# Folded statistics, transposed row spreads and split float32r sums with borrowed buffers, in a two-block kernel on one core

## The chip, the cores and the metric

One core of a Trainium2 chip runs the kernel. The metric is device time in microseconds (us). The core has a matrix engine (TensorE, PE in the profile, with its weight loads shown apart as PEld), a vector engine (VectorE, DVE), an activation engine (ScalarE, ACT), a general engine (GpSimd, POOL) and an engine that issues transfers (SyncE, SP). TensorE reads SBUF and writes PSUM.

## The reference, cut to what matters

The input is 256 tokens of 1024 features. The first block has three branches that read the same normalised input: a recurrence (RWKV), a stick-breaking attention and an attention over a memory. Their outputs are gated, projected, summed, and followed by a convolutional feed-forward part. The second block is an mLSTM layer, a feed-forward part, an attention layer and another feed-forward part. Every layer begins with an RMS norm. The lines that the change touches compute this:

```
def rms_norm(x, g, eps=NORM_EPS):
    y = x * lax.rsqrt(jnp.mean(x * x, axis=-1, keepdims=True) + eps)
    return y * g

# stick-breaking attention, per head
log_1mb = jnp.where(mask, jax.nn.log_sigmoid(-z), 0.0)
log_between = lax.cumsum(log_1mb, axis=3, reverse=True) - log_1mb
attn = jnp.where(mask, jnp.exp(jax.nn.log_sigmoid(z) + log_between), 0.0)

# merging the branches
gates = jax.nn.sigmoid(gate_logits.reshape(b, t, N_BRANCH, D_MODEL))
merged = jnp.sum(gates * jnp.einsum('btnc,ncd->btnd', ys, w_branch), axis=2)

# mLSTM: the decay matrix of a chunk is built from running sums bcum of log forget gates
dmat = jnp.where(tri, bcum[..., :, None] - bcum[..., None, :] + ib[..., None, :], -jnp.inf)
```

## The kernel before

**Layout.** Features lie on partitions, tokens on the free axis. Each weight matrix is streamed from HBM in pieces of 128 x 1024 in one fixed order. ScalarE rounds a piece to a high half in float32r (L237) and VectorE subtracts to get the low half (L238). A product of weights and activations is three float32r products, high by high, high by low and low by high (L340 to L342, or L363 to L365 where tokens lie on partitions). There are three buffers for the high and three for the low halves of pieces, so TensorE can't run further ahead in the stream than three pieces of eight 128 x 128 weight tiles. Small products that need full precision are plain float32.

**Order.** Each engine runs its own list in order. The lists are not in the order of the program text: a scheduler places the instructions by its own estimates of when operands and buffers are ready, and text that comes later fills waits of text that comes earlier. Tiles are taken from pools. A pool hands out one buffer for each tag, tiles that name the same tag share it in turn, and a tile without a tag uses its own name as the tag. A later tile's first write then waits for the last reader of the earlier tile.

**RWKV** (`run_rwkv`) keeps the operands of its chunks in the tiles `rw_sc` (SC), `rw_rb` (RB) and `rw_z` (Z). After an inversion of triangular blocks (L722, six groups) comes a loop over four chunks, each dependent on the last: products `rw_pp` with SC (L745), copies to SBUF (L748, L749), `rw_puu` with Z (L755), copies (L756, L757), the state product `rw_pS` (L764) and its scaling (L769, or L772 and L775), and products with RB into the same bank (L786). In the last chunk SC, Z and RB are read for the last time.

**Stick-breaking** runs four rounds, p = 0 to 3, each for two heads. A round computes scores `sb_z` (L896), masks them (L899), takes the softplus in `e` by three activations (L900 to L902) and a vector operation (L903), forms running sums over key positions as float32 products of `e` with a triangular constant, `sb_c` (L907 to L909), adds them to z (L910), takes the exponential (L911), multiplies by the values, `sb_o` (L916, L918), and splits the result into `yB` (L311, L312). Its working tile `sb_ze` has one buffer, so a round begins when the one before has ended.

**Gates and branches** (L927 to L940) run over n = memory, stick-breaking, RWKV, and in each over eight tiles m. One m takes a gate product of eight k (24 matmuls on `x1`) and a branch product of four k (12 matmuls on `yM`, `yB` or `yA`); k = p of `yB` comes out of round p. The weight stream has this very order, gate m, branch m, gate m + 1, and so on; the output projection and all later layers follow it.

**Statistics.** `Stats` collects squares of the stream in two 128 x 256 halves. `_rows` sums them over partitions by products with a column of ones (L429), and `_spread` brings the 1/rms of 128 tokens, a column, to a row on all partitions by a product with the identity (L440). In the mLSTM part (L1062 to L1091) `ml_pc` holds two sets of small transposes that make columns, and `ml_pm` spreads one row per head over 128 partitions by a product with four-row operands (L1086).

Of the kernel before, what the change touches and what calls it, by code (L numbers as in the profile page):

```python
# [24 lines left out]
FINE = 16  # the first pieces of weights are split by quarters: short chains share the vector engine  # L25

STARTS = (82, 148, 181, 247, 279)  # likewise the pieces where a layer starts
HEAD = 4  # tiles of an up projection that leave the last two steps of k for later


# ---------------------------------------------------------------- host layout
# [153 lines left out]
# ---------------------------------------------------------------- device side  # L185
# [5 lines left out]
def body(tc, a, out, voff, coff, tap=None, upto=99):  # L191
# [26 lines left out]
    # ---- the weight stream: [128, 1024] pieces, each split into two float32r halves  # L218
# [41 lines left out]
    # ---- inputs that stay  # L260
# [40 lines left out]
    # the tensor engine's clock comes up while the first operands arrive  # L301
# [25 lines left out]
    class Half:  # L327
        """hi and lo of 512 features in one piece"""
# [27 lines left out]
    def tp_group(X):  # L356
        """512 columns with tokens on partitions: two banks"""
        po = [ps_acc(), ps_acc()]
        for k in range(KD):
            hi, lo = W.take(4)  # L360
            for tt in range(2):
                s = slice(tt * 128, (tt + 1) * 128)
                PE.matmul(po[tt], X.H[:, k, s], hi, start=(k == 0), stop=False)  # L363
                PE.matmul(po[tt], X.L[:, k, s], hi, start=False, stop=False)  # L364
                PE.matmul(po[tt], X.H[:, k, s], lo, start=False, stop=(k == KD - 1))  # L365
        return po

    def rsqrt(v, n, name, E=V, out=None):
        """1/sqrt(v) of a small [128, n] tile, v > 0: a first guess from the exponent, a step with fitted
        constants that leaves 7e-4, then one of third order"""  # L370
        c = "r" if name[:2] == "rw" else "x"
        w = spool.tile([128, 4 * n], F32, name=name + "w", tag=f"nw{n}{c}")
        y, t, z, p = [w[:, i * n:(i + 1) * n] for i in range(4)]
        c1 = 0.703952253 * 0.375
        E.tensor_scalar(y.bitcast(I32), v.bitcast(I32), -0.5, float(0x5F1FFFF9), op0=OP.mult, op1=OP.add)
        E.tensor_tensor(t, y, y, op=OP.mult)
        E.tensor_tensor(t, t, v, op=OP.mult)
        E.tensor_scalar(t, t, -c1, c1 * 2.38924456, op0=OP.mult, op1=OP.add)
        E.tensor_tensor(z, t, y, op=OP.mult)
        E.tensor_tensor(t, z, z, op=OP.mult)  # L380
        y = out if out is not None else y
        if E is G:
            E.tensor_tensor(t, t, v, op=OP.mult)
            E.tensor_scalar(t, t, 64.0 / 9, -5.0 / 3, op0=OP.mult, op1=OP.add)
            E.tensor_tensor(p, t, t, op=OP.mult)
            E.tensor_scalar(p, p, 20.0 / 9, None, op0=OP.add)
            E.tensor_tensor(y, p, z, op=OP.mult)
        else:
            E.scalar_tensor_tensor(t, t, 64.0 / 9, v, op0=OP.mult, op1=OP.mult)
            E.scalar_tensor_tensor(p, t, -10.0 / 3, t, op0=OP.add, op1=OP.mult)  # L390
            E.scalar_tensor_tensor(y, p, 5.0, z, op0=OP.add, op1=OP.mult)
        return y

    class Stats:
        """mean of squares of a feature-major [128, 8, 256] stream, tile by tile"""
# [5 lines left out]
        def add(self, x2):  # L401
            """two tiles"""
            sq = spool.tile([128, 2, T], F32, name="st_sq", tag="st_sq", bufs=2)
            A.activation(sq, x2, AF.Square)
            if self.acc is None:
                self.acc = sq
            elif self.n == 1:
                n = spool.tile([128, 2, T], F32, name="st_acc", tag="st_acc", bufs=1)
                self.E.tensor_tensor(n, self.acc, sq, op=OP.add)
                self.acc = n  # L410
            else:
                (self.E if self.n < 3 else V).tensor_tensor(self.acc, self.acc, sq, op=OP.add)
            self.n += 1
# [10 lines left out]
        def _rows(self):  # L424
            nm = self.name
            p = ps_m("st_ps")
            for tt in range(2):
                for j in range(2):
                    PE.matmul(p[:, tt:tt + 1], self.acc[:, j, tt * 128:(tt + 1) * 128], ones[:, 0:1], start=(j == 0),  # L429
                              stop=(j == 1))  # L430
            self.v = spool.tile([128, 2], F32, name=nm + "_v", tag="st_v", bufs=4)
            V.tensor_scalar(self.v, p[:, 0:2], 1.0 / D, EPS, op0=OP.mult, op1=OP.add)
            self.rs = rsqrt(self.v, 2, nm, G, spool.tile([128, 2], F32, name=nm + "_rs", tag="st_rs", bufs=4))
            self.ev = spool.tile([128, 2], F32, name=nm + "_ev", tag="st_ev", bufs=4)
            V.tensor_scalar(self.ev, self.v, EPS, None, op0=OP.mult)

        def _spread(self):
            pb = ps_m("st_pb")
            for tt in range(2):
                PE.matmul(pb[:, tt * 128:(tt + 1) * 128], self.rs[:, tt:tt + 1].to_broadcast([128, 128]), ident,  # L440
                          start=True, stop=True)
            self.bc = spool.tile([128, T], F32, name=self.name + "_bc", tag="st_bc", bufs=2)
            A.activation(self.bc, pb[:, :T], AF.Copy)
            self.bc2 = self.bc[:, None, :].to_broadcast([128, 2, T])

    def head_rs(po, nh, ev, name):
        """rows [tok, nh heads] of two banks -> their 1/sqrt(mean + eps * v)"""
# [21 lines left out]
    def tok_to_feat(qn, dst, tt, gain):  # L469
        """[128 tok, 512] -> dst [128 feat, 4, 256] with a gain per feature"""  # L470
# [6 lines left out]
    # =============================================================== block 1  # L477
# [30 lines left out]
    # normalised already: its rows go to many places  # L508
# [10 lines left out]
    # ---- RWKV  # L519
    half_w0 = cpool.tile([128, 8], F32, name="half_w0")  # L520
    V.tensor_scalar(half_w0, vecs[:, voff["w0"][0]:voff["w0"][0] + 8], 0.5, None, op0=OP.mult)
    # -k_k, k_a / 2, 1 - k_a / 2, 1 - mu; columns of 0.5 and of the decay's factor
# [48 lines left out]
    def rw_norms():  # L571
        """1/|k| of every row and head"""
# [11 lines left out]
    def rw_prep(p, rs, SC, BK, UV, wc):  # L584
        """one pair of heads: decays, keys and values into the operands of the chunks"""
# [51 lines left out]
    def rw_scores(p, SC, BK, BA, RB, BKT, Lb):  # L637
        """scores of a pair of heads; transposes of its B, K and of its strictly lower part"""
# [23 lines left out]
    def run_rwkv():  # L662
# [17 lines left out]
        # (I - L)^-1 of all chunks and heads, both orientations  # L680
# [5 lines left out]
        # diagonal blocks of 16: one block per partition, inverted row by row  # L686
# [50 lines left out]
        # chunks  # L737
# [52 lines left out]
        # group norm  # L790
# [39 lines left out]
    # emission: first projections, half 0 as soon as its six tiles are there  # L830
# [14 lines left out]
    # ---- memory branch: attention  # L845
# [39 lines left out]
    # ---- stick-breaking branch  # L885
    skT = qk_feat(X1, None, 8, vec("sb_k"), "skT")
    sv = v_tok(X1, None, "sv")
    YB = Half("yB", "e")
    for p in range(4):
        ze = mp.tile([128, 4, 384], F32, name="sb_ze", tag="sbt")  # L890
        z, e = ze[:, 0:2], ze[:, 2:4]
        pz = [ps_m("sb_z") for _ in range(2)]
# [10 lines left out]
        V.scalar_tensor_tensor(e, z, 0.0, e, op0=OP.max, op1=OP.add)  # L903
        for par in range(2):
            ep = e[:, par]
            pc = ps_m("sb_c")
            PE.matmul(pc[:, 0:256], con("negtri"), ep[:, 0:256], start=True, stop=False, skip_group_check=True)  # L907
            PE.matmul(pc[:, 128:256], con("negtri")[:, 0:1].to_broadcast([128, 128]), ep[:, 256:384], start=False, stop=True, skip_group_check=True)
            PE.matmul(pc[:, 256:384], con("negtri"), ep[:, 256:384], start=False, stop=True, skip_group_check=True)  # L909
            V.tensor_tensor(z[:, par], z[:, par], pc[:, :384], op=OP.add)  # L910
# [12 lines left out]
    # ---- gates and branches  # L923
# [18 lines left out]
    def residual(X, gains_next, snext, Xn, kn=KD, two=False):  # L942
        """x += W X; the next layer's split input and statistics along the way"""
# [89 lines left out]
    # =============================================================== block 2: mLSTM  # L1033
# [12 lines left out]
    # log_sigmoid(f) = min(f, 0) - ln(1 + exp(-|f|))  # L1046
# [15 lines left out]
    # columns: g (by key position) and the floor of the denominator (by query position)  # L1062
    gcol = mp.tile([128, 2, 2, 4], F32, name="ml_gcol")
    pc = ps_m("ml_pc")
    pcv = pc[:, 0:16].rearrange("p (r a h) -> p r a h", r=2, h=4)
    for r in range(2):
        for tt in range(2):
            PE.transpose(pcv[:, r, tt], rows[:, r, tt * 128:(tt + 1) * 128], ident[0:4, 0:4])
# [15 lines left out]
    for h in range(4):  # L1084
        pm = ps_m("ml_pm")
        PE.matmul(pm[:, :T], ident[0:4, h:h + 1].to_broadcast([4, 128]), rows[:, 2], start=True, stop=True)  # L1086
# [79 lines left out]
    # =============================================================== block 2: attention  # L1166
# [33 lines left out]
    def mb_scores(g):  # L1200
        qT, kT = qk_[g]
        for h in range(4):
# [17 lines left out]
            # [s0,t0] [s0,t1] [s1,t1]  # L1220
# [60 lines left out]
```

## Time and profile before

| What | Value |
|---|---|
| Median of 3 runs | 1159.06 us (1157.35 to 1160.1) |
| Profiled execution, first to last instruction | 1156.9 us |
| Median of the runs less this span | 2.16 us |
| TensorE busy | 1143.2 us, 99% of the span |
| VectorE busy | 864.9 us, 75% |
| ScalarE busy | 663.7 us, 57% |
| Mean granted TensorE clock | 0.998 of full |

The profile comes from one execution; its own whole time is not listed apart from its span, so a sum made against the span is carried to the runs by the 2.16 us that lie around it. An engine's busy time is the union of its instructions' times. Matmuls overlap in the records, so the price of one is read from the distance between starts, not from its length.

### The profile page before, as it was taken

The numbers are of one execution on the slowest core, as the hardware profiler recorded it, in microseconds if no ns is written. First come the engines' busy times: TensorE is split into PE (matmuls) and PEld (weight loads), VectorE is DVE, ScalarE is ACT, GpSimd is POOL, SyncE is SP. The second block draws the span as 40 slices with busy tenths as digits, with TensorE's granted clock in tenths as the row PEclk, the third lists the DMA queues.
The fourth block names the chain that finished last, engine by engine and source line by source line (L and its number), as shares of the span: only waits on it lengthen the run. The fifth ranks groups of instructions, "written<-read, shape, count | busy, mean of one in ns | idle before, by whom it ended". The sixth has DMA issues, their size and how long they took to land.

```text
span 1156.9 us, 22629 instructions
## 1 busy us (share of the span) xinstructions
PE 1143.2 (99%) x8970; PEld 1079.9 (93%) x8970; DVE 864.9 (75%) x1636; ACT 663.7 (57%) x1132; POOL 51.7 (4%) x131
## 2 busy tenths in 40 slices
PE   8999999999999999999999999999999999999998
PEld 6897769999999999999979999999998899999998
DVE  7767877456767999866656779998669858999943
ACT  6745455364545766644546666665455656766632
POOL 2000000010001000000100010000010002000000
PEclk9999999999999999999999999999999999999999
DMA  7544333223466565666554656555655435555563
GB/s 283 183 143 130 93 101 73 93 87 114 130 222 201 169 186 183 186 176 193 165 173 132 182 166 197 185 181 174 192 190 182 152 122 168 183 182 183 182 202 109
DMA packets 60794, 189.37 MB, mean 164 GB/s; under 512 B 12688, under 2 KB 14992, under 8 KB 60688
## 3 DMA queue, kind: packets, MB, share of 16 engines
q1 hardware_dynamic: 59792, 186.51, 51.9%
q8 instruction: 70, 1.15, 0.4%
q0 software_dynamic: 320, 1.05, 0.3%
q10 hardware_dynamic: 576, 0.37, 0.1%
q14 instruction: 36, 0.29, 0.1%
HBM read 186.46 MB, written 1.44 MB: 162 GB/s over the span
## 4 chain that ended last, share of the span: by engine, by line
PE 96%; ACT 2%; DVE 1%; DMA 0%; issue 0%; SPq 0%; ACTq 0%
PE acc L340 24%; PE acc L341 24%; PE acc L342 24%; PE acc L363 4%; PE acc L364 4%; PE acc L365 4%; ACT whi L237 1%; PE tr L473 1%; PE rw_pp L745 1%; PE rw_ps L646 1%; PE rw_lt L722 1%; PE rw_lz L722 1%; PE sb_z L896 1%; PE rw_pvt L630 1%; DMA mst<-in_memT_dram 0%; PE st_ps L429 0%
## 5 line engine op out<-in xcount | busy, mean ns | idle before, releaser
L237 ACT ACTIVATE whi<-wstg 128x1024 fp32r<-128x1024 f32 (+1 forms) x453 | 374.4, 851 | 345.6 <-PE acc L341 189.3
L238 DVE TENSOR_TENSOR wlo<-wstg,whi 128x1024 fp32r<-128x1024 f32 (+1 forms) x453 | 429.6, 967 | 174.6 <-ACT whi L237 172.1
L340 PE MATMUL acc<-ffh,whi 128*128 128x256 f32 x528 | 148.5, 283 | 0.0
L341 PE MATMUL acc<-ffl,whi 128*128 128x256 f32 x528 | 148.1, 283 | 0.0
L342 PE MATMUL acc<-ffh,wlo 128*128 128x256 f32 x528 | 147.7, 283 | 0.0
L340 PEld LDWEIGHTS acc<-ffh,whi 128*128 128x128 f32 x528 | 101.2, 192 | 0.0
L341 PEld LDWEIGHTS acc<-ffl,whi 128*128 128x128 f32 x528 | 100.9, 192 | 0.0
L342 PEld LDWEIGHTS acc<-ffh,wlo 128*128 128x128 f32 x528 | 100.7, 192 | 0.0
L341 PE MATMUL acc<-x6l,whi 128*128 128x256 f32 x352 | 99.3, 284 | 0.8 <-DVE x6l L315 0.8
L340 PE MATMUL acc<-x2h,whi 128*128 128x256 f32 x352 | 99.4, 283 | 0.0
L340 PE MATMUL acc<-x6h,whi 128*128 128x256 f32 x352 | 99.3, 283 | 0.0
L340 PE MATMUL acc<-x4h,whi 128*128 128x256 f32 x352 | 99.2, 283 | 0.0
L341 PE MATMUL acc<-x2l,whi 128*128 128x256 f32 x352 | 99.2, 283 | 0.0
L341 PE MATMUL acc<-x4l,whi 128*128 128x256 f32 x352 | 99.2, 283 | 0.0
L342 PE MATMUL acc<-x2h,wlo 128*128 128x256 f32 x352 | 98.1, 283 | 0.0
L342 PE MATMUL acc<-x4h,wlo 128*128 128x256 f32 x352 | 98.1, 283 | 0.0
L342 PE MATMUL acc<-x6h,wlo 128*128 128x256 f32 x352 | 98.0, 283 | 0.0
L340 PE MATMUL acc<-x1h,whi 128*128 128x256 f32 x304 | 88.0, 291 | 2.8 <-ACT mv L496 1.9
L342 PE MATMUL acc<-x1h,wlo 128*128 128x256 f32 x304 | 87.4, 289 | 0.6 <-DVE wlo L238 0.6
L341 PE MATMUL acc<-x1l,whi 128*128 128x256 f32 x304 | 87.1, 288 | 0.0
L1007 ACT ACTIVATE ffa<-ffu,ffcv 128x256 f32<-128x256 f32 x132 | 70.8, 588 | 0.0
L341 PEld LDWEIGHTS acc<-x6l,whi 128*128 128x128 f32 x352 | 67.5, 192 | 1.2 <-DVE x6l L315 1.2
(587 smaller groups left out, 2825.1 us busy)
## 6 DMA issues: line engine op xcount, KB each, us to landing
wstg<-in_wst_dram SPq DMA_DIRECT2D x343, 512.0 KB, 3.7
wstg<-in_wst_dram SPq DMA_DIRECT2D x4, 256.0 KB, 5.2
mst<-in_memT_dram SPq DMA_DIRECT2D x4, 256.0 KB, 5.7
x<-in_xT_dram SPq DMA_DIRECT2D x2, 512.0 KB, 7.7
xt<-in_xT_dram POOLq DMA_DIRECT2D x4, 256.0 KB, 5.5
out_dram<-xt SPq DMA_DIRECT2D x8, 128.0 KB, 3.7
cst<-in_cst_dram SPq DMA_DIRECT2D x1, 673.0 KB, 8.3
small<-in_small_dram SPq DMA_DIRECT2D x1, 512.0 KB, 8.9
```

Source lines behind the costliest of these rows:

```text
L237: A.activation(hi[:, p], src[:, p], AF.Copy)
L238: V.tensor_tensor(lo[:, p], src[:, p], hi[:, p].bitcast(F32), op=OP.subtract)
L340: PE.matmul(o, hi, xh, start=start, stop=False, **kw)
L341: PE.matmul(o, hi, xl, start=False, stop=False, **kw)
L342: PE.matmul(o, lo, xh, start=False, stop=stop, **kw)
L363: PE.matmul(po[tt], X.H[:, k, s], hi, start=(k == 0), stop=False)
L364: PE.matmul(po[tt], X.L[:, k, s], hi, start=False, stop=False)
L365: PE.matmul(po[tt], X.H[:, k, s], lo, start=False, stop=(k == KD - 1))
L473: PE.transpose(p[:, j * 128:(j + 1) * 128], qn[:, j * 128:(j + 1) * 128], ident)
L630: PE.matmul(pv4[64:128, c], pv[:, c * 64:(c + 1) * 64], ident, start=True, stop=True)
L722: PE.matmul(ps[s, u], l[s, u], r[s, u], start=True, stop=True)
L1007: A.activation(ac[:, g], u[:, g, 2:], AF.Identity, scale=cv[:, c + 2:c + 3], bias=cv[:, c + 3:c + 4])
```

## The change

The sums over partitions in `_rows` are made of one half: VectorE first adds the second half of the squares to the first, and then one product per 128 tokens stands where two stood. `_spread` and the mLSTM's `ml_pm` use a TensorE transpose of a column repeated 128 times in place of a float32 product with the identity; for `ml_pm` the column of the third row set is taken from `ml_pc`, which gets two more small transposes, and a larger copy `ml_gcol`. In the stick-breaking part `e` is split into two float32r halves `eh` and `el`, the triangular constant and its first column, repeated, are copied to float32r (`ntri`, `none`), and the running sums are four float32r products: two of 384 columns and two of 128. The new tiles name tags of RWKV tiles: `sb_nr` has `rw_z`, `sb_el` has `rw_sc`, `sb_eh` has `rw_rb`. Comments and a few documentation strings go too.

```diff
         def _rows(self):
             nm = self.name
             p = ps_m("st_ps")
+            V.tensor_tensor(self.acc[:, 0], self.acc[:, 0], self.acc[:, 1], op=OP.add)
             for tt in range(2):
-                for j in range(2):
-                    PE.matmul(p[:, tt:tt + 1], self.acc[:, j, tt * 128:(tt + 1) * 128], ones[:, 0:1], start=(j == 0),
-                              stop=(j == 1))
+                PE.matmul(p[:, tt:tt + 1], self.acc[:, 0, tt * 128:(tt + 1) * 128], ones[:, 0:1], start=True, stop=True)
...
         def _spread(self):
             pb = ps_m("st_pb")
             for tt in range(2):
-                PE.matmul(pb[:, tt * 128:(tt + 1) * 128], self.rs[:, tt:tt + 1].to_broadcast([128, 128]), ident,
-                          start=True, stop=True)
+                PE.transpose(pb[:, tt * 128:(tt + 1) * 128], self.rs[:, tt:tt + 1].to_broadcast([128, 128]), ident)
...
     YB = Half("yB", "e")
+    nr = mp.tile([128, 2, 128], F32R, name="sb_nr", tag="rw_z")
+    ntri, none = nr[:, 0], nr[:, 1]
+    A.activation(ntri, con("negtri"), AF.Copy)
+    A.activation(none, con("negtri")[:, 0:1].to_broadcast([128, 128]), AF.Copy)
     for p in range(4):
         ze = mp.tile([128, 4, 384], F32, name="sb_ze", tag="sbt")
         z, e = ze[:, 0:2], ze[:, 2:4]
+        el = mp.tile([128, 2, 384], F32R, name="sb_el", tag="rw_sc")
+        eh = mp.tile([128, 2, 384], F32R, name="sb_eh", tag="rw_rb")
...
         V.scalar_tensor_tensor(e, z, 0.0, e, op0=OP.max, op1=OP.add)
+        split(eh, el, e)
         for par in range(2):
-            ep = e[:, par]
             pc = ps_m("sb_c")
-            PE.matmul(pc[:, 0:256], con("negtri"), ep[:, 0:256], start=True, stop=False, skip_group_check=True)
-            PE.matmul(pc[:, 128:256], con("negtri")[:, 0:1].to_broadcast([128, 128]), ep[:, 256:384], start=False, stop=True, skip_group_check=True)
-            PE.matmul(pc[:, 256:384], con("negtri"), ep[:, 256:384], start=False, stop=True, skip_group_check=True)
+            PE.matmul(pc[:, 0:384], ntri, eh[:, par], start=True, stop=False, skip_group_check=True)
+            PE.matmul(pc[:, 0:384], ntri, el[:, par], start=False, stop=False, skip_group_check=True)
+            PE.matmul(pc[:, 128:256], none, eh[:, par, 256:384], start=False, stop=False, skip_group_check=True)
+            PE.matmul(pc[:, 128:256], none, el[:, par, 256:384], start=False, stop=True, skip_group_check=True)
             V.tensor_tensor(z[:, par], z[:, par], pc[:, :384], op=OP.add)
...
-    gcol = mp.tile([128, 2, 2, 4], F32, name="ml_gcol")
+    gcol = mp.tile([128, 3, 2, 4], F32, name="ml_gcol")
     pc = ps_m("ml_pc")
-    pcv = pc[:, 0:16].rearrange("p (r a h) -> p r a h", r=2, h=4)
-    for r in range(2):
+    pcv = pc[:, 0:24].rearrange("p (r a h) -> p r a h", r=3, h=4)
+    for r in range(3):
...
         pm = ps_m("ml_pm")
-        PE.matmul(pm[:, :T], ident[0:4, h:h + 1].to_broadcast([4, 128]), rows[:, 2], start=True, stop=True)
+        for tt in range(2):
+            PE.transpose(pm[:, tt * 128:(tt + 1) * 128], gcol[:, 2, tt, h:h + 1].to_broadcast([128, 128]), ident)
```

## Rows read from the trace of the kernel before

**Rows 1.** The page, busy time, share of span and instructions of an engine.

```profile
PE 1143.2 (99%) x8970; PEld 1079.9 (93%) x8970; DVE 864.9 (75%) x1636; ACT 663.7 (57%) x1132; POOL 51.7 (4%) x131
```

**Rows 2.** Busy time of the engines in stretches: length, then PE, PEld, DVE, ACT, POOL (records), clock, DMA.

```profile
30.00:36.00 6.00, 4.13 (x20) 3.16 (x19) 6.00 (x21) 6.00 (x19) 0.26 (x1) 1.00 0.58 160
36.00:39.40 3.40, 3.40 (x18) 3.40 (x18) 2.51 (x10) 1.35 (x5) 1.62 (x3) 0.50 0.58 199
...
251.00:285.00 34.00, 34.00 (x335) 31.32 (x334) 19.85 (x33) 18.14 (x27) 1.84 (x2) 1.00 0.29 95
```

**Rows 3.** Tile views of `yB`, `yA`: count, shortest, median, longest (ns), first and last start.

```profile
L340 PE MATMUL acc<-yB,whi x32: 283/283/388, 260.9 to 301.1; 128*128 128x256 f32 x32
L312 DVE TENSOR_TENSOR yB<-sb_o,yB x4: 423/424/426, 202.4 to 266.8; 128x256 fp32r<-128x256 f32 x4
L342 PE MATMUL acc<-yA,wlo x32: 282/283/283, 310.9 to 339.5; 128*128 128x256 f32 x32
```

**Rows 4.** Tile views of `rw_z`, `rw_sc`, `rw_rb`: their readers in the chunk loop.

```profile
L755 PE MATMUL rw_puu<-rw_pc,rw_z x64: 218/218/267, 232.1 to 279.1; 64*64 64x64 f32 x64
L745 PE MATMUL rw_pp<-rw_uv,rw_sc x64: 218/275/323, 226.7 to 272.7; 128*128 128x64 f32 x64
L786 PE MATMUL rw_pp<-rw_uv,rw_rb x64: 218/218/267, 235.8 to 283.6; 64*64 64x64 f32 x64
```

**Rows 5.** Timeline of TensorE, running sums and the last chunk: start, length (us).

```profile
190.55 0.59 PE L907 MATMUL sb_c<-sb_ze,cst 128*128 128x256 f32 x2
191.42 0.60 PE L907 MATMUL sb_c<-sb_ze,cst 128*128 128x256 f32 x2
...
238.17 0.70 PE L907 MATMUL sb_c<-sb_ze,cst 128*128 128x256 f32 x2
...
259.16 0.65 PE L907 MATMUL sb_c<-sb_ze,cst 128*128 128x256 f32 x2
...
271.05 1.90 PE L745 MATMUL rw_pp<-rw_uv,rw_sc 128*128 128x64 f32 x16
```

**Rows 6.** Views by line of the stick-breaking round on ScalarE and VectorE.

```profile
L900 ACT ACTIVATE sb_ze<-sb_ze x4: 844/845/846, 184.1 to 250.2; 128x768 f32<-128x768 f32 x4
L902 ACT ACT_TABLE_LOAD  x4: 1283/1283/1283, 186.9 to 252.9; - x4
L903 DVE SCALAR_TENSOR_TENSOR sb_ze<-sb_ze x4: 954/958/1125, 189.1 to 255.1; 128x768 f32<-128x768 f32 x4
L910 DVE TENSOR_TENSOR sb_ze<-sb_ze,sb_c x8: 545/554/554, 191.6 to 261.2; 128x384 f32<-128x384 f32 x8
```

**Rows 7.** Groups of TensorE from 267 to 340: count, busy us, mean ns, idle.

```profile
L342 PE MATMUL acc<-x1h,wlo 128*128 128x256 f32 x107 | 30.6, 289 | 0.6 <-DVE wlo L238 0.6
```

**Rows 8.** Timeline of TensorE, a sum over partitions between products of the stream.

```profile
371.56 0.28 PE L342 MATMUL acc<-x2h,wlo 128*128 128x256 f32 x1
371.68 0.95 PE L429 MATMUL st_ps<-ones,st_acc 128*128 128x1 f32 x8
...
372.69 0.28 PE L341 MATMUL acc<-x2l,whi 128*128 128x256 f32 x1
```

**Rows 9.** Timeline of TensorE, transposes of `tok_to_feat`, and a spread.

```profile
177.15 0.60 PE L473 MATMUL tr<-cst,skTn 128*128 128x128 f32 x4
...
378.32 0.60 PE L440 MATMUL st_pb<-cst,s_rs 128*128 128x128 f32 x4
```

**Rows 10.** Timeline of TensorE in the mLSTM part.

```profile
575.76 0.28 PE L1068 MATMUL ml_pc<-cst,ml_rows 4*128 4x4 f32 x2
...
580.51 0.28 PE L342 MATMUL acc<-x3h,wlo 128*128 128x256 f32 x1
580.72 0.69 PE L1086 MATMUL ml_pm<-ml_rows,cst 4*128 4x256 f32 x2
...
581.68 0.40 PE L364 MATMUL acc<-whi,x3l 128*128 128x512 f32 x1
581.92 0.40 PE L365 MATMUL acc<-wlo,x3h 128*128 128x512 f32 x1
```

## The prediction, made before the changed kernel ran

> **What bounds the kernel now.** The page's busy table comes first: TensorE is busy for 1143.2 of 1156.9 us [rows 1]. So the time is the sum of what its instructions cost back to back, and an edit that takes TensorE work away gives its price back, provided that nothing makes TensorE wait. The second view is therefore that of stretches, to see where the cover is thin. Between 251 and 285 us TensorE is busy for all 34.00 us [rows 2]. Yet three things run there together: the last RWKV chunks, the last stick-breaking rounds and the first gates of n = 1. The tile views tell how close the last two are: `yB` is written for the last time at 266.8 + 0.4 = 267.2, while products of `yB` begin at 260.9 [rows 3]. TensorE uses `yB` as soon as it exists. What keeps it busy until then is that rounds and chunks run side by side.
>
> The third view, of the RWKV tiles, gives the last readers: Z until 279.1 + 0.2, SC until 272.7 + 0.3, RB until 283.6 + 0.2 = 283.8 [rows 4]. The running sums of round 0 start at 190.55 [rows 5], 93 us before RB is free. In the changed kernel `ntri`, `el` and `eh` lie in these three buffers, and no running sum can start without them. This is the step on which I build.
>
> **The change part by part: TensorE work that goes.** A pass of the stream with 256 columns costs 0.12 us start to start (371.56 to 371.68 [rows 8]).
>
> Statistics: from the pass before the sum (371.56) to the second pass behind it (372.69) are 1.13 us; less two passes, eight records cost 0.89 us, 0.112 each [rows 8]. Half of them go: 0.45 us for each of seven norms. The five after the start count in full, 2.2 us. The two at the start replace 0.9 us of TensorE by two VectorE additions of some 0.42 us (128 x 256, as L312 [rows 3]) where VectorE is busy for 6.00 of 6.00 us [rows 2]: 0.9 gained or 0.8 lost, taken as 0. The five other additions lie behind products of the next layer's first tiles, which don't read the statistics; without that cover each would cost 0.4 us, 2 in all.
>
> Spreads: four records serve two calls now, and four transposes take the same 0.60 us [rows 9]. So two transposes cost half, 0.22 us less per spread, 1.1 us over five.
>
> mLSTM rows: from 580.51 to 581.68 are 1.17 us; less one pass of 256 columns (0.12) and one of 512 (0.24, 581.68 to 581.92) one `ml_pm` costs 0.81 us [rows 10]. Two transposes cost 0.22, so four heads gain 2.4. The two transposes added to `ml_pc` cost up to the 0.28 of the present pair [rows 10], taken in full: net 2.1. `ml_pm` now waits for the `gcol` copy and with it for the second row set; the products of the next weights are its cover.
>
> Running sums: the two halves start 0.87 us apart [rows 5]. Float32r of 384 columns lies between 0.12 and 0.24, taken as 0.17; of 128 columns between the 0.112 of a one-column record and 0.12. Two of each make 0.57, so eight halves would gain 2.4 us. I count 0, because in my forecast TensorE is idle around them.
>
> Sum outside the stick-breaking: 2.2 + 1.1 + 2.1 = 5.4 us gained.
>
> **The wait.** What is late next follows from the weight order. TensorE can do gates m = 0 to 2 of n = 1 (they end with the third piece buffer), and then needs all four k of `yB`; k = 3 comes out of round 3. Queued behind that product are the rest of n = 1, n = 0, the output projection and all else. From 267 to the end of n = 0 TensorE now runs 107 gate passes of each kind, 13.4 gates [rows 7]. With three gates done early, 5 + 8 = 13 remain: 13 x 24 x 0.12 = 37.4 us. Of the branch with `yB` the last k of three m and five whole m remain, (9 + 60) x 0.12 = 8.3, and 96 passes with `yA`, 11.5. So n = 0 ends 57.2 us after `yB` is whole, and now it ends at 339.5 + 0.3 = 339.8 [rows 3]. The shift of all that follows is then (time of `yB`) + 57.2 - 339.8 = (time of `yB`) - 282.6.
>
> Time of `yB`, step one: when RB is free. Chunks start at 226.7 [rows 4] and, the last, at 271.05 [rows 5], so 14.8 us apart, and the last needs 283.8 - 271.1 = 12.7 more. Their bare chain is 1.9 us for 16 products with SC [rows 5], half of it (an estimate for matmuls of half the rows) for Z and for the state, and seven vector or copy steps of 256 elements, 0.42 each as L312 [rows 3]: 1.9 + 1.9 + 2.9, some 7 us. Rounds 0 to 2 no longer stand between them. Gates still do, until 247: `yB` is first used at 260.9, and TensorE is rid of some 14 us before it. (A float32 call costs 0.87 / 512 us a column [rows 5]; scores, sums and values of a round have 768 + 1024 + 768 columns, 4.4 us, and three rounds and a bit lie there.) I take 11.5 us a chunk, a start at 223, as 4 us of the 14 lie ahead of the loop, and 10 for the last: 223 + 34.5 + 10 = 268. Ends: 249 (bare chunks from 221, all but the tail in the last) and 284 (as now).
>
> Step two: a round. The split of the last result 0.4 + 0.4 [rows 3], the second half's scores 0.65 (384 columns), the mask 0.55 (as L910), three activations 0.84 each and a table load 1.28, the softplus sum 0.96 [rows 6]; new are the rounding of `e` on ScalarE, 128 x 768 as L900, 0.85, and the subtraction on VectorE, about L903's 0.96, together 1.8; then sums 1.1, addition 0.55, exponential 0.84, values 1.3 (768 columns). Bare 12.4, with an allowance of 0.1 for each of some fourteen hand-overs 14. Now a round takes 259.16 - 238.17 = 21.0 us [rows 5], with the split 22.8. I take 17, nearer to bare, since weight pieces stand still then, but RWKV's norm and output still use VectorE and ScalarE. From RB's release round 0 needs the split, sums, addition, exponential and values, 5.6 bare, taken as 7; its scores and softplus are done before. Sum: 268 + 7 + 3 x 17 + 0.8 = 327. Shift 327 - 282.6 = 44.4 us.
>
> The trace shows what an idle TensorE does to its clock: after 30 to 36 us, where it was busy for 4.13 of 6.00, the granted clock is 0.50, that is 1.2 GHz for 2.4, through 36 to 39.4 [rows 2]. In rounds TensorE would work for about 3 of 17 us, so I reckon with half clock there, 2 to 3 us more a round, and have put this into the 17.
>
> The Trainium skill, page "TensorE: Matmul & The Clock Gate", section "Why this matters for your kernels", also warns against long idle gaps between bursts, after which the array runs at half rate. By that rule the rounds would be nearer 17 than 14; the trace agrees as far as the one stretch at 36 us goes.
>
> Total: 1156.9 + 44.4 - 5.4 = 1195.9 for the profiled execution; the median of the runs lies 2.2 above its span, so 1198 us.
>
> **The rivals.** *A, buffers don't bind: faster.* If the new tiles were given memory of their own, round 0 could start as now. Each round would be 1.8 us longer, `yB` whole at 267.2 + 7.2 = 274.4, before the 282.6 from which it decides: no stall, and the gains stand, 5.4 + 2.4 = 7.8, so 1151 us. For it speaks only that RWKV's tiles give no tag of their own; against it, that a name is the tag and the pool has one buffer of each. With shared buffers the same end would need RB free by 282.6 - 49 = 234, when the second chunk has hardly begun. Chance 0.05.
>
> *B, nothing gets shorter.* RWKV ends at 284 as now and rounds keep today's pace: 284 + 9 + 3 x 22.8 + 0.8 = 362, shift 79.6, 1159.1 + 79.6 - 5.4 = 1233 us. Today's pace holds under a weight stream that would stand still. Chance 0.12.
>
> *C, all at the bare chain.* RB free at 249, rounds of 14: 249 + 6 + 42 + 0.8 = 298, shift 15, 1159.1 + 15 - 5.4 = 1169 us. Gates fill TensorE until about 247, which speaks against bare chunks before that. Chance 0.13.
>
> The Trainium skill, page "Perfetto Trace Analysis", section "Optimization Strategy", says that the same gap repeating on an engine that should be saturated can mean that there is no room for the next tile. That is the mechanism of the forecast, against A; the trace of before has no such gap (34.00 of 34.00 us busy [rows 2]), so nothing here confirms it yet.
>
> **How the numbers follow.** The forecast, a stall of 25 to 65 us, has 0.68 and gives 1180 to 1217 by itself. With B and C, 0.93 are slower; 0.05 faster is A; 0.02 within 0.2% (2.3 us, about what a measurement of this kernel can tell from no change) is A with its gains eaten by longer rounds. The range leaves out A and the far ends of B and C: 1173 to 1230.
>
> **What would show it.** Right: no `sb_c` before the last L786; TensorE nearly idle from about 250 for some 60 to 80 us but for RWKV and four repeated rounds, waits of `yB` products for the split of round 3, granted clock 0.50 there; then the same work as now, shifted; sums over partitions, spreads and `ml_pm` cheaper by 0.45, 0.22 and 0.6 us a time. Wrong: running sums before RB is free (A), rounds of 14 or 22 us (C, B), or chunks that don't come faster without the rounds between them.

## The result, and the profile after

The changed kernel takes 1203.24 us (1202.11 to 1203.8) where the kernel before, on the same chip, takes 1159.03 (1157.35 to 1160.1): the ratio is 1.0385, with a 95% interval of 1.0371 to 1.0398. The profiled execution spans 1200.3 us.

The page of the changed kernel, busy time, and TensorE, granted clock and DMA in 40 slices of 30 us:

```profile
PE 1158.2 (96%) x8918; PEld 1088.9 (91%) x8918; DVE 871.0 (73%) x1647; ACT 667.7 (56%) x1138; POOL 53.8 (4%) x131
...
PE   8999999977699999999999999999999999999998
...
PEclk9999999975599999999999999999999999999999
DMA  8544324210056656565555466665566544666663
```

The first line has TensorE busier than before [rows 1], with 52 instructions fewer. That is no contradiction: the clock line falls in three slices, and at half the clock the same instruction lasts longer. The loss lies in one place, near 250 to 340 us, where DMA shows 1, 0, 0: the weight stream stands still. By stretches (columns as in [rows 2]):

```profile
226.00:251.00 25.00, 24.38 (x252) 22.57 (x250) 9.89 (x17) 7.54 (x13) 2.47 (x4) 1.00 0.32 102
251.00:285.00 34.00, 27.50 (x205) 21.98 (x205) 17.72 (x36) 12.95 (x22) 0.00 (x0) 0.55 0.01 4
285.00:340.00 55.00, 36.42 (x168) 29.39 (x168) 21.15 (x33) 23.56 (x28) 0.00 (x0) 0.60 0.11 33
340.00:390.00 50.00, 50.00 (x419) 50.00 (x419) 31.65 (x49) 23.86 (x36) 2.36 (x4) 1.00 0.63 191
```

From 251 to 285 TensorE was busy for 34.00 us before [rows 2]; now it is for 27.50, at a clock of 0.55, with 205 records for 335. Its two largest waits between 251 and 345 (total, times, longest):

```profile
PE sb_c L911 <- ACT sb_eh L311: 12.0, 3, 5.3
PE sb_o L921 <- ACT sb_ze L916: 8.3, 4, 3.7
```

The tile views come next, to be held against [rows 3] and [rows 4] (columns as there). That of `rw_z` and of `sb_nr`, which follows in its buffer:

```profile
L753 PE MATMUL rw_puu<-rw_pc,rw_z x64: 217/219/367, 228.9 to 261.9; 64*64 64x64 f32 x64
...
L889 ACT ACTIVATE sb_nr<-cst x1: 309/309/309, 262.3 to 262.3; 128x128 fp32r<-128x128 f32 x1
```

Those of `rw_sc`, read for the last time at 260.2, and of `rw_rb`:

```profile
L743 PE MATMUL rw_pp<-rw_uv,rw_sc x64: 221/275/443, 224.1 to 259.7; 128*128 128x64 f32 x64
...
L784 PE MATMUL rw_pp<-rw_uv,rw_rb x64: 218/268/367, 233.2 to 264.0; 64*64 64x64 f32 x64
```

That of `sb_eh`, which follows in RB's buffer, with the running sums that read it:

```profile
L911 PE MATMUL sb_c<-sb_eh,sb_nr x8: 522/606/690, 265.7 to 318.8; 128*128 128x384 f32 x8
...
L311 ACT ACTIVATE sb_eh<-sb_ze x4: 842/842/843, 264.8 to 317.4; 128x768 fp32r<-128x768 f32 x4
```

And those of `yB` and of `yA`:

```profile
L312 DVE TENSOR_TENSOR yB<-sb_o,yB x4: 423/424/425, 272.7 to 324.6; 128x256 fp32r<-128x256 f32 x4
```

```profile
L342 PE MATMUL acc<-yA,wlo x32: 283/283/283, 356.3 to 388.1; 128*128 128x256 f32 x32
```

Z is read until 262.2 and `sb_nr` written at 262.3; RB is read until 264.4 and `sb_eh` written at 264.8. The first running sum starts at 265.7, and before it was 190.55 [rows 5]. `yB` is whole at 324.6 + 0.4 = 325.0 and the last product with `yA` ends at 388.1 + 0.3 = 388.4, 48.6 us later than before [rows 3]. The whole span grew by 43.4 us; so some 5 us came back behind that point.

### The profile page after: what moved, and what is told of

The parts are those of the page before. It is cut to its first block, busy times and chain, and to the rows that moved or that the text cites. A ratio compares the mean times of both kernels' runs of the same rounds, so it can differ in the third digit from the quotient of the medians.

```text
span 1200.3 us, 22552 instructions
## 1 busy us (share of the span) xinstructions
PE 1158.2 (96%) x8918; PEld 1088.9 (91%) x8918; DVE 871.0 (73%) x1647; ACT 667.7 (56%) x1138; POOL 53.8 (4%) x131
## 4 chain that ended last, share of the span: by engine, by line
PE 92%; ACT 4%; DVE 2%; issue 1%; POOL 0%; DMA 0%; SPq 0%; ACTq 0%; POOLq 0%; DVEq 0%
PE acc L340 23%; PE acc L341 23%; PE acc L342 23%; PE acc L365 4%; PE acc L363 4%; PE acc L364 4%; PE sb_z L900 1%; PE rw_pp L743 1%; ACT whi L237 1%; PE tr L471 1%; PE rw_ps L644 1%; PE rw_lz L720 1%; PE rw_lt L720 1%; DVE wlo L238 1%; PE rw_pvt L628 0%
```

## Experiments

The theory: the three borrowed buffers, each last read in RWKV's last chunk, make the whole loss, and the rest of the change gains some 5 us. A rival is that the new operations (split, float32r sums) lengthen the rounds whatever the buffers, or that one buffer alone (the large RB) makes the wait and the 1 KB of constants none.

**The same work in free buffers.** The three tiles take buffers of tags that nothing else holds then; `el` becomes two tiles.

```diff
-    nr = mp.tile([128, 2, 128], F32R, name="sb_nr", tag="rw_z")
+    nr = mp.tile([128, 2, 128], F32R, name="sb_nr", tag="qn", bufs=2)
-        el = mp.tile([128, 2, 384], F32R, name="sb_el", tag="rw_sc")
-        eh = mp.tile([128, 2, 384], F32R, name="sb_eh", tag="rw_rb")
+        el = [mp.tile([128, 384], F32R, name="sb_el", tag="t2", bufs=2) for _ in range(2)]
+        eh = mp.tile([128, 2, 384], F32R, name="sb_eh", tag="s4a")
```

> The whole change, but the three new tiles of the stick-breaking part lie in buffers that are free before round 0: eh in that of the memory keys (4 KB, last read near 165 us), el as two tiles in the two buffers of the memory probabilities, the constants in one of the two buffers of the normed queries. Theory (the stall comes from the wait for RWKV's buffers): no stall, and the gains stand, 5.4 us outside the stick-breaking and up to 2.4 in it: 1151 to 1154 us, running sums of round 0 near 193 us. Rival 1 (the stall comes from the longer round, with the rounding and the subtraction on the way): still slower than before, 1165 us or more. Rival 2 (rounds are longer, and yB is late by 7 us more than TensorE has other work for): 1154 to 1165 us.

Measured 1154.65 us (1153.18 to 1156.17), ratio 0.9966 (0.9953 to 0.9979). The tile view of `sb_eh` in this kernel, and then that of `rw_rb`:

```profile
L913 PE MATMUL sb_c<-sb_eh,sb_nr x8: 337/339/442, 196.4 to 262.9; 128*128 128x384 f32 x8
```

Readers of RB:

```profile
L784 PE MATMUL rw_pp<-rw_uv,rw_rb x64: 217/218/268, 241.5 to 284.4; 64*64 64x64 f32 x64
```

All eight halves are summed before RB is free at 284.6, and no stall is left: `yB` is whole at 269.1, before the 282.6 of the prediction, and TensorE's waits between 251 and 345 are 0.8 and 0.6 us, neither of them for `yB`. So the second rival's mechanism falls too, although the time lies in its range. The whole loss, 48.6 us against this kernel, hangs on where three tiles lie. The gain, however, is 4.2 us and not the expected 5 to 8.

**One borrowed buffer at a time.** First only the constants stay in `rw_z`, with `eh` and `el` free as above.

> As the run with buffers of their own, but the two 128 x 128 constants (1 KB a partition) stay in the buffer of rw_z, as in the change. Theory: one borrowed constant is enough. The last product with Z starts at 261.9 us in the changed kernel, so running sums can begin near 263, with the split of round 0 already made: 2 us earlier than in the change, and from then on the same rounds: 1199 to 1203 us. Rival (RB, the last buffer to come free, and the large SC make the stall): 1155 us or less.

Measured 1197.51 us, ratio 1.0337 (1.0322 to 1.0353), a little under the expected range: rounds 2 and 3 took 13.9 and 15.8 us, where the same rounds as in the changed kernel (16.2 each) had been taken. Z is read until 264.1 there, and then the constants are written:

```profile
L889 ACT ACTIVATE sb_nr<-cst x1: 309/309/309, 264.2 to 264.2; 128x128 fp32r<-128x128 f32 x1
```

The second run is the kernel before, with no new operation at all, only `e` in RB's buffer:

```diff
-        z, e = ze[:, 0:2], ze[:, 2:4]
+        z = ze[:, 0:2]
+        e = mp.tile([128, 2, 384], F32, name="sb_e", tag="rw_rb")
```

> The kernel before, with one edit: the softplus tile e (128 x 768, float32) is a tile of its own in the buffer of rw_rb, in place of the second half of the working tile. No operation is added or changed. Theory: activations of round 0 now wait for the last reader of RB. RB free near 265, then round 0 from its first activation (some 12 us), three rounds of some 15.5 us (no rounding, no subtraction), yB whole near 325: a shift of some 45 us without any gain, 1198 to 1210 us. Rival (the new operations make the stall, not the buffer): 1159 us, as before.

Measured 1209.1 us, ratio 1.0438 (1.0422 to 1.0453). The tile views of `rw_rb` and of `sb_e` there:

```profile
L786 PE MATMUL rw_pp<-rw_uv,rw_rb x64: 218/218/366, 231.5 to 261.6; 64*64 64x64 f32 x64
```

The first write of `e`, and the sums that read it:

```profile
L901 ACT ACTIVATE sb_e<-sb_ze x4: 842/842/844, 262.3 to 314.6; 128x768 f32<-128x768 f32 x4
...
L908 PE MATMUL sb_c<-sb_e,cst x16: 634/634/794, 267.3 to 321.9; 128*128 128x256 f32 x16
```

So a tile of constants, 128 x 256 and written once, stalls the kernel nearly as the whole change does, and so does one tile of the old kernel without any of the new operations. Both rivals fall: the new operations don't make the loss, and RB isn't needed for it. The buffer of Z alone is enough, and so is that of RB. SC's was not tried alone; it comes free at 260.2 in the changed kernel, Z at 262.2 and RB at 264.4.

**The change without its stick-breaking part.**

> The change without its stick-breaking part: folded statistics, spreads by transposes, and the mLSTM rows. Theory: TensorE's work alone gets shorter, 2.2 us by the statistics, 1.1 by the spreads, 2.1 in the mLSTM part: 1159.0 - 5.4 = 1153.6, between 1152.5 and 1155. Rival (the additions on VectorE and the wait of ml_pm for more columns take it back): 1157 to 1160.

Measured 1155.95 us (1154.14 to 1158.15), ratio 0.9975 (0.9965 to 0.9986): 2.9 us gained, 5.3 expected. From the last product with `yA` to the last with the last layer's input it takes 744.8 us where the kernel before takes 750.5, so the 5.2 us of that stretch (four spreads, five sums, the mLSTM rows) are there, even 5.7. The loss lies ahead of it: the last product with `yA` ends at 343.4 there, at 339.8 before.

**Is half the clock what makes a round long?** Eight float32 products of `z` with the identity are added to each round, read by nobody.

```diff
+        pd = ps_r("sb_warm")
+        for _ in range(4):
+            for par in range(2):
+                PE.matmul(pd[:, 0:384], ident, z[:, par], start=True, stop=True)
```

> The changed kernel with eight more float32 products of 384 columns in each stick-breaking round, of the masked scores with the identity, into a bank that nobody reads. They add work to TensorE while it waits for ScalarE and VectorE, and change no result. Theory (6 us of the shift are the half clock: rounds with slow products, and the first 8 us after yB is whole at 0.50): the granted clock stays or comes back to 1.00 for most of the rounds and the resumption, rounds get 1 to 2 us shorter and the tail behind yB some 4 us: 1192 to 1199 us. Rival (the clock sets nothing, the chain through ScalarE and VectorE does): 1202 to 1204. If the added products stand in the way of the running sums, 1204 to 1212.

Measured 1208.12 us, ratio 1.0436 (1.0417 to 1.0456): the expectation failed, in the branch it names. The timeline of TensorE in round 0 (start, length):

```profile
269.19 0.41 PE L918 MATMUL sb_c<-sb_el,sb_nr 128*128 128x128 f32 x1
275.03 1.98 PE L811 MATMUL rw_py<-cst,rw_krv 128*64 128x64 f32 x32 [5.43 <-DVE rw_krv L800]
...
281.27 5.43 PE L907 MATMUL sb_warm<-sb_ze,cst 128*128 128x384 f32 x16 [0.28 <-ACT rw_yo L821]
288.22 0.66 PE L925 MATMUL sb_o<-sb_ze,sv 128*64 128x256 f32 x4 [1.52 <-ACT sb_ze L920]
```

The engine's list puts RWKV's output products, which wait 5.43 us for VectorE, and the added products ahead of the values `sb_o` of round 0; `yB`'s first write ends at 290.0 for 273.1. Behind that the clock part can be seen: the writes of rounds 1 to 3 follow at 13.1, 14.7 and 13.1 us, where the changed kernel needs 19.6, 16.2 and 16.2. Their granted clocks are 0.97, 0.79 and 0.96, against 0.59, 0.50 and 0.50. Round 3 with the added products, and in the changed kernel (columns as in [rows 2]):

```profile
317.80:330.90 13.10, 10.01 (x44) 6.32 (x44) 4.42 (x7) 7.16 (x8) 0.00 (x0) 0.96 0.00 0
```

```profile
308.90:325.00 16.10, 8.76 (x30) 6.16 (x29) 4.54 (x7) 7.16 (x8) 0.00 (x0) 0.50 0.00 0
```

Rounds 2 and 3, when RWKV is gone in both, are 1.5 and 3.1 us shorter although they hold more work, and the one that had the higher clock is the shorter one. As the added products also move other work, this is not a test of the clock alone.

**Does the order of the gates make the stall expensive?** RWKV's gates and products before stick-breaking's (in the text, and the host's weight order follows it), so that n = 0 covers the rounds; two operand pairs change places to fit.

```diff
-    for n, Yn in ((2, YM), (1, YB), (0, YA)):
+    for n, Yn in ((2, YM), (0, YA), (1, YB)):
```

> The changed kernel with the gates and branches in the order memory, RWKV, stick-breaking (weights in HBM in that order too), so that the products of yB stand last; the output projection's input takes the slots of yM and yA in place of yM and yB. Buffers are borrowed as in the change. Theory (the stall lasts until yB is whole because all later weights are queued behind its products): RWKV's output is there at 288 us in the changed kernel, so TensorE has the third group of gates and branches to do while rounds 1 to 3 run. yB whole at 325 to 330, then five gates and the branch products of n = 1, 23 us: 348 to 355 in place of 388.4, so 1163 to 1172 us. Rival (what sets the end is not the place of yB's products in the weight order): 1195 us or more.

Measured 1181.23 us, ratio 1.0198 (1.0181 to 1.0215): half of the loss goes, less than expected.

```profile
L340 PE MATMUL acc<-yB,whi x32: 278/283/386, 328.4 to 367.3; 128*128 128x256 f32 x32
...
L312 DVE TENSOR_TENSOR yB<-sb_o,yB x4: 417/423/425, 274.0 to 340.4; 128x256 fp32r<-128x256 f32 x4
```

The work behind the last write falls from 63.3 to 27.1 us, but `yB` is whole only at 340.8: the rounds now run under the weight stream, and the writes lie 18.5, 25.5 and 22.4 us apart, the pace of the kernels without a stall (20.0, 25.4 and 18.7 with free buffers). I had left them at the pace that they have under a stream that stands still.

**The start.** In the kernel with free buffers and in the one without the stick-breaking part the first product with `x1` starts at 37.3 and 37.5 us, before at 35.6. The two norms at the start get their two products per 128 tokens back; all other norms stay folded. Once with the free buffers, once without the stick-breaking part; beside them the stick-breaking part alone, in free buffers, in the kernel before.

```diff
+            nj = 2 if nm in ("sm", "s1") else 1
+            if nj == 1:
-            V.tensor_tensor(self.acc[:, 0], self.acc[:, 0], self.acc[:, 1], op=OP.add)
+                V.tensor_tensor(self.acc[:, 0], self.acc[:, 0], self.acc[:, 1], op=OP.add)
```

> The change with the running sums' tiles in buffers that are free, as in the earlier run of that kind (1154.65 us), and with the two norms at the start summed as in the kernel before: two products per 128 tokens, no addition on VectorE. All else of the change stands. Theory (the additions lie on the path of the start, where VectorE is busy throughout, and drag ScalarE's copy and POOL's small steps with them): the first product of the stream with x1 comes back from 37.3 to between 35.3 and 36.0 us, and the time falls by 1.5 to 2 us, to 1152.5 to 1153.5. Rival (the start varies with the placement of instructions or with the clock, the additions are innocent): first product with x1 still at 36.7 to 37.5, time 1154 to 1155.5.

> The change without its stick-breaking part, as in the earlier run of that kind (1155.95 us), and with the two norms at the start summed as in the kernel before. Theory: as beside it, the first product with x1 at 35.3 to 36.0 us and 1153.5 to 1154.5 us, near the 1153.6 of the sum of the prediction's terms (5.4 less than before). Rival: 1155.2 to 1156.5.

> The kernel before with the stick-breaking part of the change alone: the split of e, the float32r sums, the copied constants, all in free buffers; statistics, spreads and the mLSTM rows as before. The prediction's term: eight halves gain 0.30 us of TensorE each, 2.4 us in all where TensorE is the bound, so 1155.8 us against 1158.2 before. Rival (each round is longer by the split, and the two more copies and eight more instructions on the vector engines take back what TensorE saves): 1157.5 to 1159.5.

The first measured 1151.11 us (1150.27 to 1153.46), ratio 0.9933 (0.9921 to 0.9946), the fastest of all; the second 1152.95 (1151.19 to 1154.56), 0.9948 (0.9935 to 0.9961). The kernel before stood at 1158.74 beside them and at 1158.86 beside the earlier two, so putting the old sums back gains 3.5 and 3.0 us, more than either theory said. The place that I named is not shown: the first product with `x1` is at 36.4 and 38.1, not at 35.3 to 36.0, and POOL's chain is as slow without the additions (9.16 us busy from 14 to 30, with them 9.21, before 6.91), so they don't drag it. TensorE does wait for that chain, 1.0 us in the kernel with free buffers and 1.9 in both with the old sums, and not in the kernel before. With free buffers and the old sums (total, times, longest):

```profile
PE st_pb L443 <- POOL s_rs L387: 1.9, 1, 1.9
```

So part of what the start loses is not the additions' doing. What does differ is seen by stretches (columns as in [rows 2]) in the kernels with free buffers. With the additions:

```profile
30.00:50.00 20.00, 17.69 (x129) 16.48 (x127) 16.01 (x45) 15.22 (x43) 1.89 (x3) 1.00 0.54 166
...
172.00:185.00 13.00, 12.04 (x81) 11.02 (x79) 10.17 (x42) 5.80 (x11) 0.00 (x0) 0.87 0.14 42
```

Without them:

```profile
30.00:50.00 20.00, 19.39 (x140) 18.07 (x139) 17.48 (x53) 16.13 (x47) 1.89 (x3) 1.00 0.58 182
172.00:185.00 13.00, 12.64 (x98) 11.87 (x99) 11.74 (x39) 5.87 (x11) 0.00 (x0) 1.00 0.13 40
```

With the additions TensorE works less from 30 to 50 us, though over 0 to 50 the difference is only 42.34 to 42.93; and one stretch of 3.4 us at half clock is there in one execution and not in the other. The third kernel, which has the sums of the kernel before, has such a stretch too (0.87 from 172 to 185), so it isn't tied to the additions alone. By the same products of the stream, the kernel without the additions is 0.9 us ahead from 84 to 166 us in both pairs of traces (first `rw_ps` product at 84.3 and 83.4, at 86.0 and 85.1), and 2.2 and 2.5 us ahead at the last product with `yA` (339.8 and 337.6, 343.4 and 340.9). So most of the difference arises behind the start: in the first pair with the half-clock stretch at 172 to 185, in the second between 190 and 250, where TensorE's list has another order. Why either comes with the additions stays open.

The third measured 1157.39 us (1155.74 to 1170.05), ratio 0.9992 (0.9969 to 1.0014): 1.4 us, with an interval that holds no change and also the 2.4 of the term. By medians the parts add up: 5.8 and 1.4 make 7.2, and together they gain 7.6.

## Why the prediction was right, step by step

**The mechanism: right.** No running sum ran before the last product with RB, four rounds stood alone, the clock fell to half in them, and all later work was shifted. The experiments show the cause as one of buffers: free ones end the stall, and one borrowed one alone brings it back, for Z's and RB's.

**RB free: 268 forecast, 264.4 measured.** Chunks start at 224.1, 237.9, 249.8 and 256.5, so they are 13.8, 11.9 and 6.7 apart, and the last needs 7.9. The gates run until 250 and slow the first two, as taken; the last two run bare, the last of them at a granted clock of 0.50. The bare 7 of the working was right, and the 10 for the last too long.

**Round 0: 7 forecast, 8.8 measured** (264.4 to 273.1). The trace has RWKV's mean and subtraction on VectorE between the split and the addition.

**Rounds: 17 forecast, 17.3 measured** ((325.0 - 273.1) / 3). Two things in it were not as worked out. Each of the last three rounds has a second table load on ScalarE, which the sum did not hold:

```profile
298.07 1.28 ACT L906 ACT_TABLE_LOAD   x1
299.37 0.84 ACT L906 ACTIVATE sb_ze<-sb_ze 128x768 f32<-128x768 f32 x1
301.24 0.84 ACT L311 ACTIVATE sb_eh<-sb_ze 128x768 fp32r<-128x768 f32 x1 [1.02 <-DVE sb_ze L907]
302.10 1.28 ACT L916 ACT_TABLE_LOAD   x1
```

Before, in three of the four rounds that second load stood at the gates' tanh (L932) and once at the exponential (L911); now the exponential pays it, on the chain. And half the clock goes with some 3 us a round by the run with added products (13.1 us near full clock, 16.2 at 0.50), where 2 to 3 was reckoned. Without the clock the working has 14 where 13.1 were measured with that load in it, so its allowances were too large; round 1, with RWKV in it, took 19.6 and brings the mean near 17. Part of this hit is luck. So `yB` was whole at 325.0, 327 forecast: 3.6 us early, then 1.8 and 0.9 late, and the 0.8 for the last split is already in the measured rounds; together the 1.8 from 326.8 to 325.0. That the terms offset each other is luck as well.

**The work behind `yB`: 57.2 forecast, 63.3 measured.** This is the term that was mis-sized, and the whole miss of 4.4 us in the span (1195.9 to 1200.3) is this term's 6.1 less the 2 us above, and 0.3 in the gains up to the end of the span. It was priced at 0.12 us a pass. TensorE in the changed kernel, on both sides of 333 us:

```profile
332.41 0.41 PE L340 MATMUL acc<-x1h,whi 128*128 128x256 f32 x1
332.62 0.41 PE L341 MATMUL acc<-x1l,whi 128*128 128x256 f32 x1
...
333.47 0.28 PE L340 MATMUL acc<-x1h,whi 128*128 128x256 f32 x1
333.59 0.28 PE L341 MATMUL acc<-x1l,whi 128*128 128x256 f32 x1
```

Starts are 0.21 us apart and then 0.12: the clock that the rounds had lost comes back only at 332.9, 7.9 us after `yB` is whole. Thirty passes start before that, each 0.093 us dearer: 2.8 us. Waits for the gates and for weights right after the stall are 1.5 us. The remaining 1.8 are passes that the working left out: 492 start between 325.0 and 388.4 where it has 477 (312 of gates, 69 with `yB`, 96 with `yA`; 300, 76 and 96 start, and 20 of the output projection stand ahead of the last with `yA`). The runs with one borrowed buffer have the same tail, 62.6 (383.8 - 321.2) and 62.8 us (389.5 - 326.6).

**The gains outside the stick-breaking: 5.4 in all, 5.2 of it behind `yA`; there 5.4 measured** (750.5 to 745.1, up to the last product with the last layer's input). In the changed kernel:

```profile
420.46 0.28 PE L342 MATMUL acc<-x2h,wlo 128*128 128x256 f32 x1
420.58 0.50 PE L429 MATMUL st_ps<-ones,st_acc 128*128 128x1 f32 x4
420.94 0.36 PE L340 MATMUL acc<-x2h,whi 128*128 128x256 f32 x1
...
644.19 0.38 PE L1092 MATMUL ml_pm<-cst,ml_gcol 128*128 128x128 f32 x2
644.33 0.48 PE L363 MATMUL acc<-whi,x3h 128*128 128x512 f32 x1
```

A sum costs 0.48 - 0.12 = 0.36 us for the 0.89 of [rows 8], and an `ml_pm` 0.14 from start to start for 0.81 [rows 10]: both somewhat more gain than forecast. The cover held; no product waited for an addition there.

**The two norms at the start: taken as 0, measured as 3 to 3.5 us lost** by putting the old sums back. The lower bound, 0.8 lost, was too small: it priced the additions alone, and only 0.9 of the loss is there by 166 us. With the stall present this changed the forecast little, but without it that one term would have eaten nearly half of the gain.

**The running sums: 0 in the forecast, 2.4 without a stall; 1.4 measured alone**, not told apart from either.

**Rival A's figure.** 1151 us for buffers that don't bind: the change with free buffers gives 1154.65, and 1151.11 once the start is as before. **B and C** fell on the rounds, 17.3 for 22.8 and 14, and on the chunks, of which two were slow and two bare.

## What to carry to other kernels

A tile put into another's buffer adds a wait for that tile's last reader: look up in the trace when that reader runs and what is queued behind the first use, before counting what the new operations save. A small tile is no safer: 128 x 256 of constants, written once, cost nearly as much here as all three tiles. Buffers that came free some 70 us after the first use was due turned 4 us of gain into 44 of loss. An addition that takes work off TensorE isn't free everywhere: at the start of this kernel, where VectorE is busy for 6.00 of 6.00 us [rows 2], the kernels with two of them were 3.0 and 3.5 us slower, though the two save 0.9 us of TensorE by the prediction's price; how most of that comes about is not settled.

## What the runs showed of the hardware

After this stall the granted clock stayed at 0.50 for another 7.9 us, in which TensorE was busy for 7.2, before it rose; in the runs with one borrowed buffer it stayed for 6.1 and 6.8 us and with the added products for 5.7. So the price of this stall went on behind its end, by 2.8 us. The loads of activation tables moved to other lines: with the gates gone from between two steps of the round, a load of 1.28 us came onto the chain (four loads at L906, three at L916 and one at the gates' L937, where before there were four at L902, one at L911 and three at the gates' L932). POOL's small steps between 14 and 30 us took 9.0 to 9.2 us in all in the kernels with the changed spreads, with and without the additions, and 6.9 before and with the stick-breaking part alone; why is not settled.
